# Computing the products with w_up by seven block products instead of eight

## The chip, the core and the metric

The kernel runs on one core of one Trainium2 chip. A core has a matrix engine (TensorE, PE in the profile, with its weight loads as PEld), three engines for elementwise work (VectorE or DVE, ScalarE or ACT, GpSimd or POOL) and a queue that starts the transfers (SyncE or SP). Each engine works off its own list of instructions in order and waits at semaphores for the others. Matrix products are written to PSUM, which has eight banks of 128 partitions x 512 float32; TensorE reads its operands from SBUF. The metric is the time of one execution in device microseconds, lower is better.

## What is computed

One layer of a decoder trunk on 512 tokens of width 1024, all in float32: two gated mixers (a convolution module and a sparse attention), a channel mixer, an embedding gate and a final norm. The change is in the channel mixer:

```
D_MODEL = 1024; SEQ = 512; D_FF = 2816
...
x = x + y @ w_out[i]
hf = rmsnorm(x, norm_ffn[i])
up = causal_dwconv(hf @ w_up[i], ffn_dw_w[i], ffn_dw_b[i])     # w_up: (1024, 2 * 2816), a conv of three taps
gate, val = jnp.split(up, 2, axis=-1)
x = x + (jax.nn.gelu(gate) * val) @ w_down[i]
```

`hf @ w_up` has 512 rows and 5632 columns, that is 44 chunks of 128 columns: 22 of gates (f) and 22 of values (22 + f).

## The kernel before

**Products in two parts.** A product of float32 operands is made from parts: each operand is cut into a `hi` part (a copy rounded to the engine's float32r, by ACT, helper `hi_of`, line 107) and a `lo` part (what is left, by DVE, helper `lo_of`, line 110). Three matmuls then stand for one: hi x hi, hi x lo, lo x hi (`mm_w` at lines 117 to 119 with the weights as the stationary operand, `mm_a` at 123 to 125 with the activations as the stationary operand).

**The weights' stream.** Weights arrive in pieces of 128 x 1024 float32 (512 KB) in the order of their use. `Stream.pump` asks for the next pieces (two raw buffers, `wraw`, started from SP) and starts to cut those that were asked for earlier, into one of four buffers `whl`. `Stream.work` runs the next stage of a cut, `take` hands a cut piece to the products, `done` gives its buffer back. So cuts of later pieces stand in ACT's and DVE's lists between the evacuations of earlier products.

**Around the channel mixer.** `rows_product` makes 512 x 1024 results as row tiles of 128 tokens (t) and column halves (n); `residual` adds them to the rows `x2`. With w_out, the second half runs row tile by row tile: after a tile's product comes its norm (`Norm`: squares on ACT, the power on POOL, the scaled row `hrow` on DVE), and one tile later eight transposes on TensorE (`to_T`, line 341) whose two results of 128 x 512 are cut into `hfT`. After the last tile a product with w_ple (`ple_half`, 24 matmuls) stands between its norm and its transposes.

**The channel mixer.** `up_chunk` (line 1161) makes one chunk of 128 columns for all 512 tokens: eight k steps of three matmuls of 512 columns into one bank. ACT takes it out with the conv's last tap and its bias (line 1170), DVE adds the two other taps, which read the bank (1171, 1172). For a pair, a gate's chunk and a value's, there follow gelu (ACT, 1180), the product (DVE, 1182) and the cut of the result into `a`. Pairs run in groups of 8, 8 and 6; after a group the product with its rows of w_down is made. POOL has nothing to do in the channel mixer.

Of the kernel before, what the change touches and what calls it, by code (L numbers as in the profile page):

```python
# [11 lines left out]
F32R = mybir.dt.float32r  # L12
# [29 lines left out]
# heads whose scores, two units ahead, and whose weights, one unit ahead, are due in a unit's steps  # L42
# [41 lines left out]
def block_kernel(ctx: ExitStack, tc: tile.TileContext, x, p, rel_bias, norm_mix, w_in, conv_dw_w, conv_dw_b,  # L84
# [9 lines left out]

    ctx.enter_context(tc.manual_schedule())
# [4 lines left out]
    def work(name, shape, dtype=F32, tag=None, bufs=1):  # L100
        return sb.tile(list(shape), dtype, name=name, tag=tag or name, bufs=bufs)
# [7 lines left out]
    def lo_of(dst, src, hi):  # L109
        nc.vector.tensor_tensor(dst, src, f32(hi), op=ALU.subtract)  # L110
# [4 lines left out]
    # out += W.T a  with W's parts as the stationary operand  # L115
# [5 lines left out]
    # out += a.T W  with the activations' parts as the stationary operand  # L121
# [6 lines left out]
    # A piece lands as fp32 and is cut into an exact (hi, lo) pair of float32r parts, some pieces ahead of its use.  # L128
# [7 lines left out]

    def rows_pieces(name, w, ks):
        for n in range(2):
            for i in range(0, len(ks), 2):
                nk = len(ks[i:i + 2])  # L140
                pieces.append(((name, n, ks[i]), [cols(w, ks[i], nk, 512 * n, 512)], nk, 512, "whl"))

    def ple_piece(n):
        pieces.append((("ple", n), [cols(w_ple, 0, 2, 512 * n, 512)], 2, 512, "accX"))
# [8 lines left out]
    CMP_AFTER = CMP_AT                      # the compression's eight pieces follow the z pieces from this one on  # L153
# [9 lines left out]
    rows_pieces("out", w_out, list(range(KC)))  # L163
    FFN_GROUPS = ((0, 8), (8, 16), (16, NF))
    for f0, f1 in FFN_GROUPS:
        for f in range(f0, f1):
            for c in (f, NF + f):
                pieces.append((("up", c), [cols(w_up, 0, KC, c * P, P)], KC, P, "whl"))
        if f1 == NF:
            ple_piece(1)  # L170
        rows_pieces("down%d" % f0, w_down, list(range(f0, f1)))
# [4 lines left out]
    class Stream:  # L176
        limit, parts = CUT, 1
        dmas = cuts = taken = raws = wholes = hls = call = 0

        def __init__(self):  # L180
            self.raw, self.hl, self.asked, self.stages = {}, {}, {}, []

        def pump(self, force=False):
# [3 lines left out]
            while self.cuts < self.dmas and (force or self.asked[self.cuts] < self.call):  # L187
                i = self.cuts
                key, _, a, b, tag = pieces[i]
                if tag is not None:  # L190
# [6 lines left out]
                    self.raws -= 1  # L197
                self.cuts += 1
            while self.dmas < len(pieces):
                i = self.dmas  # L200
                key, srcs, a, b, tag = pieces[i]
                if (self.wholes if tag is None else self.raws) == 2:
                    break
                raw = work("wraw", (P, a, b), tag="pT" if tag is None else "wraw", bufs=2)
# [6 lines left out]
                self.raws += tag is not None  # L211
# [21 lines left out]
        def take(self, *key):  # L233
            i = self.taken
# [1049 lines left out]
```

## Time and profile before

| | |
|---|---|
| time, median of 3 runs | 837.78 us (837.27 to 838.08) |
| span of the profiled execution | 835.6 us (its own time beside the span is not given apart; the median lies 2.2 us above the span) |
| TensorE's granted clock | at its full level in all 40 slices of the page |
| matmuls | 3872, of these 1056 with w_up |

The page gives each engine's busy time. A matmul's own duration is longer than the distance to the next, since they are pipelined, so what one costs in a row of many is read from the starts of the first and the last. An engine's idle time is put down to what released it. Transfers ran at a mean of 101 GB/s, and in no wait of TensorE in the channel mixer was a transfer named.

### The profile page before, as it was taken

The page shows a single profiled execution, that of the slowest core. Times are in us where ns is not written, and L with a number is a line of the kernel's source. Part 1 is how long each engine was busy: PE and PEld are TensorE (multiplying, and loading weights), DVE is VectorE, ACT ScalarE, POOL GpSimd, SP SyncE. Part 2 cuts the span into 40 slices and gives each one's busy share as a digit, 9 for nine tenths or more (in the row PEclk, how much of TensorE's full clock was granted, in tenths as well). Part 3 has the DMA queues.
Part 4 walks back from the last instruction along what each step waited for, and adds up shares of the span by engine and source line. Part 5 has one row for each costly group of instructions (what it writes and reads, how often), then busy time and mean ns, then how long its engine had stood idle before and what let it go on. Part 6 is the DMA issues. An engine that isn't in the chain of part 4 may idle for free.

```text
span 835.6 us, 10144 instructions
## 1 busy us (share of the span) xinstructions
PE 821.3 (98%) x3872; PEld 669.0 (80%) x3872; DVE 539.6 (65%) x907; ACT 375.4 (45%) x677; POOL 24.7 (3%) x71
## 2 busy tenths in 40 slices
PE   7999999999999999999999999999999999999996
PEld 6888888888888886888788888888888888888885
DVE  6379977988987897935566663355654356655564
ACT  6332524287778874432544441234442123433443
POOL 2000000000010000001000000000000000001012
PEclk9999999999999999999999999999999999999999
DMA  7347787411110116430333324232333323341312
GB/s 217 83 112 202 165 188 173 96 51 51 51 51 27 51 52 219 134 101 26 100 101 102 93 85 125 80 94 81 99 100 102 101 75 102 102 147 55 120 32 101
DMA packets 108026, 84.54 MB, mean 101 GB/s; under 512 B 4080, under 2 KB 93608, under 8 KB 107978
## 3 DMA queue, kind: packets, MB, share of 16 engines
q1 hardware_dynamic: 107978, 83.90, 35.5%
q8 instruction: 30, 0.49, 0.3%
q14 instruction: 18, 0.15, 0.1%
HBM read 79.36 MB, written 2.43 MB: 98 GB/s over the span
## 4 chain that ended last, share of the span: by engine, by line
PE 96%; ACT 1%; DVE 1%; DMA 1%; issue 0%; POOL 0%; SPq 0%; POOLq 0%; ACTq 0%
PE ps L117 19%; PE ps L119 19%; PE ps L118 19%; PE ps L123 9%; PE ps L124 9%; PE ps L125 9%; PE ps L759 2%; PE ps L785 2%; PE ps L565 2%; PE ps L704 1%; PE ps L705 1%; PE ps L341 1%; PE ps L713 1%; DMA vraw<-in_w_in 1%; PE ps L803 0%
## 5 line engine op out<-in xcount | busy, mean ns | idle before, releaser
L110 DVE TENSOR_TENSOR whl<-wraw,whl 128x1024 fp32r<-128x1024 f32 (+1 forms) x159 | 155.6, 987 | 146.8 <-ACT whl L107 143.7
L107 ACT ACTIVATE whl<-wraw 128x1024 fp32r<-128x1024 f32 (+1 forms) x159 | 133.7, 862 | 124.2 <-PE ps L125 94.3
L117 PE MATMUL ps<-hfT,whl 128*128 128x512 f32 x352 | 139.1, 395 | 0.3 <-ACT hfT L107 0.3
L118 PE MATMUL ps<-hfT,whl 128*128 128x512 f32 x352 | 139.1, 395 | 0.2 <-DVE hfT L110 0.2
L119 PE MATMUL ps<-hfT,whl 128*128 128x512 f32 x352 | 139.0, 395 | 0.0
L117 PE MATMUL ps<-hT,whl 128*128 128x512 f32 x256 | 102.8, 402 | 0.0
L119 PE MATMUL ps<-hT,whl 128*128 128x512 f32 x256 | 101.1, 395 | 0.3 <-DVE whl L110 0.3
L118 PE MATMUL ps<-hT,whl 128*128 128x512 f32 x256 | 100.9, 394 | 0.0
L625 DVE SCALAR_TENSOR_TENSOR acc<-aT,convw,acc 128x512 f32<-128x512 f32 x120 | 86.2, 746 | 1.0
L118 PEld LDWEIGHTS ps<-hfT,whl 128*128 128x128 f32 x352 | 66.2, 188 | 16.4 <-DVE hfT L110 0.5
L117 PEld LDWEIGHTS ps<-hfT,whl 128*128 128x128 f32 x352 | 66.2, 188 | 16.2 <-ACT hfT L107 0.5
L119 PEld LDWEIGHTS ps<-hfT,whl 128*128 128x128 f32 x352 | 66.2, 188 | 15.9
L123 PE MATMUL ps<-whl,a 128*128 128x512 f32 x176 | 69.7, 396 | 0.0
L125 PE MATMUL ps<-whl,a 128*128 128x512 f32 x176 | 69.5, 395 | 0.0
L124 PE MATMUL ps<-whl,a 128*128 128x512 f32 x176 | 69.5, 395 | 0.0
L1170 ACT ACTIVATE up<-ps,ffnw 128x512 f32<-128x512 f32 x44 | 34.3, 780 | 61.5 <-PE ps L119 61.5
L1171 DVE SCALAR_TENSOR_TENSOR up<-ps,ffnw,up 128x511 f32<-128x511 f32 x44 | 33.0, 750 | 43.9 <-ACT up L1170 43.8
L119 PEld LDWEIGHTS ps<-hT,whl 128*128 128x128 f32 x256 | 48.2, 188 | 12.0 <-DVE whl L110 0.7
L117 PEld LDWEIGHTS ps<-hT,whl 128*128 128x128 f32 x256 | 48.2, 188 | 9.9 <-issue 0.2
L118 PEld LDWEIGHTS ps<-hT,whl 128*128 128x128 f32 x256 | 48.3, 189 | 9.4
L125 PEld LDWEIGHTS ps<-whl,a 128*128 128x128 f32 x176 | 33.0, 188 | 8.0
L123 PEld LDWEIGHTS ps<-whl,a 128*128 128x128 f32 x176 | 33.1, 188 | 7.9
(191 smaller groups left out, 1263.6 us busy)
## 6 DMA issues: line engine op xcount, KB each, us to landing
wraw<-in_w_up SPq DMA_DIRECT2D x44, 512.0 KB
wraw<-in_w_in SPq DMA_DIRECT2D x32, 512.0 KB
wraw<-in_w_down SPq DMA_DIRECT2D x22, 512.0 KB
wraw<-in_w_out SPq DMA_DIRECT2D x8, 512.0 KB
wraw<-in_w_ple_gate SPq DMA_DIRECT2D x8, 512.0 KB
W<-vdram SPq DMA_DIRECT2D x8, 264.0 KB
xin<-in_x SPq DMA_DIRECT2D x4, 512.0 KB
wraw<-in_w_ck SPq DMA_DIRECT2D x4, 512.0 KB
```

What stands on the lines that cost most here:

```text
L107: nc.scalar.activation(dst, src, AF.Copy, scale=scale)
L110: nc.vector.tensor_tensor(dst, src, f32(hi), op=ALU.subtract)
L117: nc.tensor.matmul(o, hl[:, 0, j, cs], a_hi, start=start, stop=False)
L118: nc.tensor.matmul(o, hl[:, 0, j, cs], a_lo, start=False, stop=False)
L119: nc.tensor.matmul(o, hl[:, 1, j, cs], a_hi, start=False, stop=stop)
L123: nc.tensor.matmul(o, a_hi, w_hi, start=start, stop=False)
L124: nc.tensor.matmul(o, a_hi, w_lo, start=False, stop=False)
L125: nc.tensor.matmul(o, a_lo, w_hi, start=False, stop=stop)
L565: nc.tensor.matmul(hid_ps[kv][hf], raw[:, jj, hf * P:(hf + 1) * P], Xw[kv][j // 8][:, :, s0:s0 + 16 * (NCMP - 1) + 1:16], start=j == 0, st ...
L625: nc.vector.scalar_tensor_tensor(acc[:, c, :], a[:, k:k + S], convw[:, 4 * k + c:4 * k + c + 1], acc[:, c, :], op0=ALU.mult, op1=ALU.add)
L1170: nc.scalar.activation(u, o, AF.Identity, scale=fw(2, c), bias=fw(3, c))
L1171: nc.vector.scalar_tensor_tensor(u[:, 1:], o[:, :S - 1], fw(1, c), u[:, 1:], op0=ALU.mult, op1=ALU.add)
```

## The change

Two chunks of a pair, a gate's and a value's, are seen as one product of 2 x 2 blocks: the tokens in two halves of 256, the 1024 inner elements in two halves of 512, and the two chunks as the columns. Plain, it has eight block products. Strassen's form (in Winograd's arrangement) has seven, named m1 to m7, and takes sums as operands:

- of the activations: s1 = a21 + a22, s2 = s1 - a11 (DVE), s3 = a11 - a21, s4 = a12 - s2 (POOL), where a21 is the second token half's first inner half. They are made once, on rows, before the transposes. Instead of two transposed results for each of four row tiles there are two for each of tiles 0 and 1 and five for each of tiles 2 and 3.
- of the weights, for every pair: t1 and t2 (`add` "a"), t4 and t3 (`add` "b"), four subtractions of 128 x 512 on POOL. A pair's two raw pieces of 512 KB give four pieces to cut: "11" (128 x 1024), "t12", "t34" (sums, 128 x 1024 each) and "22" (128 x 512, whose `lo` part is made by POOL, but for two of the pairs).
- of the results: a block product that is needed in several outputs is made once, and ACT copies the partial sum between PSUM banks, or between halves of one, before other block products are added: copies after m1, m6, m7 and a "seed" of the gate's bank, 128 x 256 each; m5's result goes to SBUF (`e`), and DVE adds it to both halves of the value (`v`).

A block product is four k steps of three matmuls of 256 columns. A pair in the loop's steady state has the slots m6, m2, m1 of the next pair, m7, m5 of the next pair, m3, m4. Behind each slot stands a stage of a weight's cut and a step of the earlier pair's evacuation (`after`): the two chunks' taps, gelu, product and cut. The value's two taps now read `v` in SBUF, and its first tap too. The copies' waits: m7 waits for the copy of m6 (two slots between), m4 for that of m7 (two slots), m2 for the seed (three slots), m6 for the copy of m1.

The groups are now 7, 7 and 8 pairs, and a group's product with w_down comes inside the second pair after it. Gates and values keep two banks each for all pairs, so four banks are left for the rest. Buffers of the mixers and of the channel mixer are now in two pools, one after the other. The piece of w_ple is asked for after w_out's.

Core of the diff (the bookkeeping of buffers, the loop's first pair and the last stage's changed names are left out):

```diff
+    def mm_block(o, hl, j0, a, start):
+        for k in range(4):
+            nc.tensor.matmul(o, hl[:, 0, j0 + k, :], a[:, 0, k, :], start=start and k == 0, stop=False, skip_group_check=True)
+            nc.tensor.matmul(o, hl[:, 0, j0 + k, :], a[:, 1, k, :], start=False, stop=False, skip_group_check=True)
+            nc.tensor.matmul(o, hl[:, 1, j0 + k, :], a[:, 0, k, :], start=False, stop=k == 3, skip_group_check=True)
...
-    FFN_GROUPS = ((0, 8), (8, 16), (16, NF))
+    FFN_GROUPS = ((0, 7), (7, 14), (14, NF))
...
+    for f in range(1, NF):
+        if f + 1 < NF:
+            up_raw(f + 1)
+            up_sums(("a", f + 1), ("b", f + 1), ("11", f + 1))
...
+        up_sums(("t34", f))
+        if f + 1 < NF:
+            up_sums(("t12", f + 1))
+        up_sums(("22", f))
...
+                    self.cut(hl, src, a, nc.gpsimd if key[0] == "22" and key[1] not in DOWN_IN else nc.vector)
...
+            sub = lambda to, x_, y_: nc.gpsimd.tensor_tensor(to, x_, y_, op=ALU.subtract)
+            if name == "a":
...
+                sub(t1, at("12"), at("11"))
+                sub(t2, at("22"), t1)
...
+            else:
+                sub(to[:, 4:8], at("21"), at("t2"))
+                sub(to[:, 0:4], at("22"), at("12"))
...
+        nc.vector.tensor_tensor(s1, a21, a22, op=ALU.add)
+        nc.vector.tensor_tensor(s2, s1, a11, op=ALU.subtract)
+        nc.gpsimd.tensor_tensor(s3, a11, a21, op=ALU.subtract)
+        nc.gpsimd.tensor_tensor(s4, a12, s2, op=ALU.subtract)
...
+        def m1(self):
+            self.b1 = st.take("11", self.f)
+            mm_block(self.extra[:, HI], self.b1, 0, hf["a11"], True)
+            nc.scalar.activation(self.value[:, HI], self.extra[:, HI], AF.Copy)
+        def seed_gate(self):
+            nc.scalar.activation(self.gate[:, LO], self.value[:, HI], AF.Copy)
+        def m5(self):
+            self.t12 = st.take("t12", self.f)
+            mm_block(self.extra[:, LO], self.t12, 0, hf["s1"], True)
+            self.e = work("m5", (P, 256), tag="sc", bufs=2)
+            nc.scalar.activation(self.e, self.extra[:, LO], AF.Copy)
+        def m6(self):
+            mm_block(self.value[:, HI], self.t12, 4, hf["s2"], False)
+            nc.scalar.activation(self.value[:, LO], self.value[:, HI], AF.Copy)
+        def m2(self):
+            mm_block(self.gate[:, LO], self.b1, 4, hf["a12"], False)
+        def m7(self):
+            self.t34 = st.take("t34", self.f)
+            mm_block(self.value[:, HI], self.t34, 0, hf["s3"], False)
+            nc.scalar.activation(self.gate[:, HI], self.value[:, HI], AF.Copy)
+        def m3(self):
+            b22 = st.take("22", self.f)
+            mm_block(self.value[:, LO], b22, 0, hf["s4"], False)
+        def m4(self):
+            mm_block(self.gate[:, HI], self.t34, 4, hf["a22"], False)
...
+            nc.vector.tensor_tensor(halves(v), halves(self.value), self.e.unsqueeze(1).broadcast_to((P, 2, 256)),
+                                    op=ALU.add)
...
+            nc.scalar.activation(ug, self.gate, AF.Identity, scale=fw(2, f), bias=fw(3, f))
+            yield
+            nc.scalar.activation(uv, v, AF.Identity, scale=fw(2, c), bias=fw(3, c))
+            self.taps(ug, self.gate, f)
+            yield
+            nc.scalar.activation(ug, ug, AF.Gelu_apprx_tanh)
+            self.taps(uv, v, c)
```

How the lists stand. First DVE's, for one pair in the middle of the channel mixer; `whl` are weights' cuts (the `lo` part), `up` the two chunks' taps, `a` the cut of the pair's result. Before:

```order
L110 TENSOR_TENSOR whl_4585<-wraw_4525,whl_4585 128x1024
L1171 SCALAR_TENSOR_TENSOR up_4615<-ps_4589,ffnw0_816,up_4615 128x511
L1172 SCALAR_TENSOR_TENSOR up_4615<-ps_4589,ffnw0_816,up_4615 128x510
L110 TENSOR_TENSOR whl_4620<-wraw_4554,whl_4620 128x1024
L1171 SCALAR_TENSOR_TENSOR up_4650<-ps_4624,ffnw0_816,up_4650 128x511
L1172 SCALAR_TENSOR_TENSOR up_4650<-ps_4624,ffnw0_816,up_4650 128x510
L1182 TENSOR_TENSOR up_4650<-up_4615,up_4650 128x512
L110 TENSOR_TENSOR a_4655<-up_4650,a_4655 128x512
```

The same place now; `tt` are the weights' sums, `ug` and `uv` the gate's and the value's chunk, `m5` the result of m5 in SBUF:

```order
L121 TENSOR_TENSOR whl_5597<-wraw_5343,whl_5597 128x1024
L121 TENSOR_TENSOR whl_5614<-tt_5416,whl_5614 128x1024
L121 TENSOR_TENSOR whl_5630<-tt_5541,whl_5630 128x1024
L121 TENSOR_TENSOR a_5591<-uv_5465,a_5591 128x512
L1359 SCALAR_TENSOR_TENSOR ug_5594<-ps_3344,ffnw0_819,ug_5594 128x511
L1359 SCALAR_TENSOR_TENSOR ug_5594<-ps_3344,ffnw0_819,ug_5594 128x510
L1359 SCALAR_TENSOR_TENSOR uv_5593<-v_5595,ffnw0_819,uv_5593 128x511
L1359 SCALAR_TENSOR_TENSOR uv_5593<-v_5595,ffnw0_819,uv_5593 128x510
L1379 TENSOR_TENSOR uv_5593<-ug_5594,uv_5593 128x512
L1366 TENSOR_TENSOR v_5723<-ps_3345,m5_5575 128x512
```

Eight instructions a pair have become ten: a third cut of 128 x 1024 and the sum `v` have come, and the value's two taps read SBUF (`v`) where they read a bank (`ps`).

POOL's list has no row in the channel mixer before. Now it has these for every pair; here they are for one pair, and the first of the next:

```order
L307 TENSOR_TENSOR tt_5541<-wraw_5393,wraw_5343 128x512
L307 TENSOR_TENSOR tt_5541<-wraw_5393,tt_5541 128x512
L307 TENSOR_TENSOR tt_5544<-wraw_5343,tt_5541 128x512
L307 TENSOR_TENSOR tt_5544<-wraw_5393 128x512
L121 TENSOR_TENSOR whl_5647<-wraw_5265,whl_5647 128x512
L307 TENSOR_TENSOR tt_5669<-wraw_5521,wraw_5471 128x512
```

Five two-operand instructions of 128 x 512 a pair have come to POOL, all with both operands in SBUF. ACT's list for a pair went from six instructions (two cuts of 128 x 1024, two takings-out, gelu, the cut of `a`) to thirteen: the cut of "11", of "t34", m6's copy, the cut of "t12", the gate's taking-out, the cut of "22", m1's copy, the value's first tap, m7's copy, gelu, m5's copy, the seed, the cut of `a`, in this order.

## Rows read from the trace of the kernel before

**Rows 1.** The page: span, and each engine's busy time, share and instructions
```profile
span 835.6 us, 10144 instructions
...
PE 821.3 (98%) x3872; PEld 669.0 (80%) x3872; DVE 539.6 (65%) x907; ACT 375.4 (45%) x677; POOL 24.7 (3%) x71
```

**Rows 2.** Waits of PE, 380 to 836: in total, times, longest (us)
```profile
PE ps L117 <- ACT hfT L107: 0.3, 1, 0.3
PE ps L118 <- DVE hfT L110: 0.2, 1, 0.2
```

**Rows 3.** Windows: busy us (instructions) per engine, clock, DMA share, GB/s
```profile
560.00:650.00 90.00, 90.00 (x387) 72.39 (x386) 51.46 (x60) 33.90 (x42) 0.00 (x0) 1.00 0.32 96
```

**Rows 4.** Timeline of PE, w_up products: start, duration, line, operands
```profile
560.04 0.39 PE L118 MATMUL ps<-hfT,whl 128*128 128x512 f32 x1
...
574.98 0.39 PE L119 MATMUL ps<-hfT,whl 128*128 128x512 f32 x1
```

**Rows 5.** Timeline of PE, 256-column products at the end
```profile
822.08 0.28 PE L123 MATMUL ps<-whl,hpT 128*128 128x256 f32 x1
...
827.65 0.28 PE L125 MATMUL ps<-whl,hpT 128*128 128x256 f32 x1
```

**Rows 6.** Timeline of PE, a row tile's transposes (L341) between products
```profile
383.50 1.03 PE L341 MATMUL ps<-ci,hrow 128*128 128x128 f32 x8
384.29 0.47 PE L123 MATMUL ps<-whl,y 128*128 128x512 f32 x1
384.61 0.39 PE L124 MATMUL ps<-whl,y 128*128 128x512 f32 x1
```

**Rows 7.** Lines by form, 500 to 836: busy us, mean ns, idle before
```profile
L110 DVE TENSOR_TENSOR whl<-wraw,whl 128x1024 fp32r<-128x1024 f32 x56 | 68.5, 1224 | 94.2 <-ACT whl L107 94.1
...
L107 ACT ACTIVATE whl<-wraw 128x1024 fp32r<-128x1024 f32 x55 | 57.8, 1052 | 85.0 <-PE ps L125 84.1 <-DMA wraw<-in_w_down 1.0
...
L1170 ACT ACTIVATE up<-ps,ffnw 128x512 f32<-128x512 f32 x28 | 21.8, 780 | 40.1 <-PE ps L119 40.1
...
L1171 DVE SCALAR_TENSOR_TENSOR up<-ps,ffnw,up 128x511 f32<-128x511 f32 x28 | 21.0, 750 | 28.6 <-ACT up L1170 28.5
...
L1137 DVE TENSOR_TENSOR x<-ps,x 128x512 f32<-128x512 f32 x24 | 16.1, 686 | 7.6 <-PE ps L125 7.6
...
L110 DVE TENSOR_TENSOR a<-up,a 128x512 fp32r<-128x512 f32 x14 | 9.7, 693 | 9.8 <-ACT a L107 9.8
...
L107 ACT ACTIVATE a<-up 128x512 fp32r<-128x512 f32 x14 | 8.9, 633 | 32.6 <-DVE up L1182 32.6
...
L1180 ACT ACTIVATE up<-up 128x512 f32<-128x512 f32 x14 | 8.8, 632 | 23.2 <-DVE up L1172 23.2
...
L1207 ACT ACTIVATE pg<-ps 128x256 f32<-128x256 f32 x2 | 0.7, 374 | 0.4 <-PE ps L125 0.4
```

**Rows 8.** Timeline of POOL: small operations of the norms
```profile
757.52 0.21 POOL L318 TENSOR_SCALAR ss<-ss 128x1 f32<-128x1 f32 x1 [1.15 <-ACT junk L314]
...
807.79 2.86 POOL L318 TENSOR_SCALAR ss<-ss 128x1 f32<-128x1 f32 x4 [27.30 <-ACT junk L314]
...
814.13 0.63 POOL L327 TENSOR_TENSOR rstd<-ss 128x1 f32<-128x1 f32 x1 [3.48 <-ACT junk L314]
```

**Rows 9.** Timeline of DVE beside them
```profile
757.39 0.69 DVE L1137 TENSOR_TENSOR x<-ps,x 128x512 f32<-128x512 f32 x1 [0.71 <-PE ps L125]
...
808.70 2.49 DVE L1250 TENSOR_TENSOR x<-x,gain 128x512 f32<-128x512 f32 x4
...
814.02 0.69 DVE L1221 TENSOR_TENSOR x<-x,gain 128x512 f32<-128x512 f32 x1 [0.85 <-ACT junk L314]
```

**Rows 10.** Lines by form of POOL, whole span: its two widest memsets
```profile
L510 POOL MEMSET VC<- 32x256 f32 x1 | 0.3, 303 | 0.0
...
L509 POOL MEMSET KCt<- 128x128 f32 x1 | 0.2, 205 | 0.0
```

More of the change, by code (lines that the diff above doesn't have):

```diff
@@ L233, in take @@
         def take(self, *key):
+            while pieces[self.taken][4] in ("first", "second", "add"):
+                self.taken += 1
             i = self.taken
             assert pieces[i][0] == key, (pieces[i][0], key)
-            if i == self.cuts - 1:
+            if i >= self.cuts - 2:
                 while self.stages:
@@ L1065, in block_kernel @@
     yT = {}
-    x2 = work("x2", (P, NT, D), tag="B", bufs=2)
-    for t in range(NT):
-        nc.sync.dma_start(x2[:, t, :], x_rows[t])
     for m2 in range(4):
@@ L1107, in rows_product @@
                 between()
-            for t in range(NT):
+            before = None
+            for t in order:
                 if t == NT - 1 and last:
@@ L1147, in block_kernel, with ready, out_done @@
     gain_f = load_gain(norm_ffn)
-    hfT = work("hfT", (P, 2, KC, S), F32R, tag="A", bufs=1)
-    hl_ple = st.take("ple", 0)
     for t in range(NT):
         p_parts(t)
+    for t in range(NT):
+        nc.sync.dma_start(x2[:, t, :], x_rows[t])
+    pairs = {}
+    def ready(t):
+        norms[t].rows(halves=True)
+        row_sums(t)
+    def out_done(t, n, o):
+        residual(t, n, o, gain_f)
+        if n and t != 3:
+            ready(t)
+        if n and t == 1:
+            st.adds = 1
@@ new lines, in out_late, with before_last @@
+    def out_late(t):
+        turn_halves(t, ROWS_FIRST if t == 2 else EVERY)
+        if t == 1:
+            turn_halves(2, ("s3", "s4", "a22"))
+    def before_last():
+        ready(3)
+        st.adds = len(pieces)
+        st.pump()
+        ple_half(0)
+        st.work()
+        st.pump()
+        pairs[0] = Pair(0)
+        pairs[0].m1()
+        st.work()
+        st.pump()
+        turn_halves(3, ("s1",))
+        pairs[0].seed_gate()
+        pairs[1] = Pair(1)
+        pairs[1].m1()
+        st.work()
+        st.pump()
+        turn_halves(3, ("s2",))
+        pairs[1].seed_gate()
@@ new lines, in block_kernel, with step, slot, down @@
+                 banks=lambda n, t: (gates + values)[t] if n else ps(), order=(0, 2, 1, 3), cut_on=True)
+    tails = []
+    def step():
+        for tail in list(tails):
+            if next(tail, tails) is tails:
+                tails.remove(tail)
+    def slot(product, cut=True):
+        product()
+        st.work()
+        step()
+        if cut:
+            st.pump()
+    def down(f0, f1, gain, *late, **kw):
+        rows_product("down%d" % f0, list(range(f0, f1)),
+                     lambda k, t: (act[k][:, 0, t * P:(t + 1) * P], act[k][:, 1, t * P:(t + 1) * P]),
+                     lambda t, n, o: residual(t, n, o, gain), *late, **kw)
@@ new lines, in drain @@
+    def drain():
+        while tails:
+            step()
+    for f in range(NF):
+        this, coming = pairs[f], pairs.get(f + 1)
+        if f == 0:
+            slot(this.m5)
+            turn_halves(3, ("s3",))
+            slot(coming.m2)
+            slot(this.m6)
+            turn_halves(3, ("s4",))
+            slot(coming.m5)
+            turn_halves(3, ("a22",))
+            slot(this.m7)
+            slot(this.m2)
+        else:
+            cut = f not in DOWN_IN
+            slot(this.m6, cut)
+            if f > 1:
+                slot(this.m2, cut)
+            else:
+                step()
+            if f + 1 < NF:
+                coming = pairs[f + 1] = Pair(f + 1)
+                slot(coming.m1, cut)
+            if f in DOWN_IN:
+                step()
+                st.pump(most=1)
+                step()
+                st.work()
+                drain()
+                down(*DOWN_IN[f], None, banks=lambda n, t: ps() if t < 3 else coming.gate)
+            slot(this.m7)
+            if f + 1 < NF:
+                slot(coming.m5)
+                coming.seed_gate()
+        tails.append(this.after())
+        slot(this.m3)
+        slot(this.m4)
@@ L1199, in block_kernel @@
+    drain()
+    gain_p = load_gain(norm_ple)
+    hpT = [work("hpT", (P, 2, KC, P), F32R, tag="hf", bufs=7) for t in range(NT)]
+    down(*FFN_GROUPS[-1], gain_p, lambda t: norms[t].to_T(hpT[t], 0), lambda: ple_half(1))
     gain_o = load_gain(norm_final)
```

272 lines of the change are left out of this document (188 added, 84 removed).

## The prediction

> **What bounds the kernel now.** I read the engines' busy time first, then what TensorE waited for, then a stretch of the channel mixer, then the timeline of single instructions. TensorE is busy for 98% of the span [rows 1]; the reader is to see that no other engine comes near. From the last norm of the mixers to the end it waited in two places, 0.5 us together, both where the transposed rows are first cut [rows 2]. In 90 us of the w_up stage it was busy for all 90, at a granted clock of 1.00 (the 2.4 GHz level), with DVE at 51.5, ACT at 33.9 and POOL at nothing [rows 3]. So this stage takes what its matmuls take, one after the other, and only what shortens that row, or makes it wait, changes the time.
>
> **The matmuls.** 512 columns: 64 steps from 560.04 to 574.98, 0.2334 us each [rows 4]. 256 columns: the last tile of the final product has 48 of them in a row with a new weight for each; 47 steps from 822.08 to 827.65 are 0.1185 us each [rows 5], which is 0.508 of the long one, so loading a weight for every 256 columns is hidden. Removed: 44 chunks x 24 = 1056 x 0.2334 = 246.5 us. Added: 22 pairs x 7 x 12 = 1848 x 0.1185 = 219.0 us. **-27.5 us**. A pair falls from 11.20 to 9.95 us, a slot is 1.42.
>
> **The transposes.** Eight take 0.79 us (383.50 to 384.29), and the product behind them needs 0.32 to its next where 0.23 is usual [rows 6]: 0.88 for eight, 0.44 for a set of four. Sets go from 8 to 14: **+2.6 us**, all on TensorE.
>
> **The entry.** Behind the last row tile of w_out's product the norm's chain is longer by two DVE sums of 0.69 (the 128 x 512 form of [rows 7]); beside them stand two new m1 slots, 2.84 us, in addition to the 24 matmuls with w_ple that cover the chain today but for 0.5 us [rows 2]. Between nothing and 2.8 (both sums and a first cut, late in full); I take **+1.0**.
>
> **The copies.** I set a pair at 0 with its m6 and put ACT's thirteen instructions in their order with the durations of [rows 7] (1.052 a cut of 128 x 1024, 0.633 one of 128 x 512, 0.780 a taking-out, 0.632 gelu, 0.374 for 128 x 256 out of a bank, the nearest row for a copy into one). The cut of "t34" begins when m4 of the pair before gives its buffer back, at 0, and ends at 1.1; m6's copy runs 1.5 to 1.9, m7 needs it at 4.26. The cut of "t12" ends at 2.95, its `lo` part on DVE (1.224) at 4.2, m5 needs it at 5.69. Gate out to 3.7, cut of "22" to 4.4; m1's copy to 4.7; value's tap to 5.5; m7's copy to 6.1, needed by m4 at 8.53; gelu to 6.8; m5's copy to 7.5, seed to 7.9, `a` to 8.5, and the cut of the next "11" follows. That is 8.48 us of work in 9.95, and no product is kept waiting: the least room is 2.3 us for a copy and 1.5 for a cut. **0** while ACT isn't held up; what it costs when it is, is a rival below. Four free banks in place of eight for w_down's products: a bank is emptied by one DVE add (0.686 [rows 7]) while the other tiles' last products run; nothing, or up to 2 us over three groups. Transfers: the same bytes, 96 GB/s in [rows 3] becomes 108, no wait for one today; nothing. The order of pieces on SP's queue changes (x2 and w_ple later), with a whole product ahead of their use; nothing.
>
> **DVE and POOL.** DVE's ten instructions a pair: 3 x 1.224 + 4 x 0.750 + 2 x 0.693 + 0.686 = 8.74 us of 9.95 (before 6.83 of 11.20). That fits alone. But POOL now works beside it, and the two touch: a POOL operation of one element takes 0.21 us while DVE adds from a bank to SBUF; the same form takes 2.86 us for four while DVE multiplies two SBUF operands, and one that begins at 814.13 during such a DVE instruction ends at 814.76, just behind its end at 814.71 [rows 8, 9]. So POOL stands still while DVE reads two operands from SBUF. The other direction no row shows: DVE's four keep 0.6 us from one to the next, but POOL's work there is one element.
>
> By that, port time adds up. DVE's share with two SBUF operands is 3 x 1.224 + 2 x 0.750 (the value's taps, which now read `v`) + 2 x 0.693 = 6.56 us a pair. POOL's five two-operand instructions of 128 x 512 have no row. Bounds: memsets of 256 and 128 elements differ by 98 ns, 0.77 ns an element on top of 0.106 us [rows 10]; one such stream of 512 is 0.50 us, three one after the other (two reads, a write) 1.29. The nearest row of the same form is DVE's 0.693, which I take: 6.56 + 5 x 0.69 = 10.0 us, just over TensorE's 9.95. As the pieces won't fit without gaps I add 0.25 us a pair: **+5.5 us**. At 0.50 the sum is 9.06 and it costs nothing; at 1.29 it is 13.0 and costs 3.05 x 22 = 67.
>
> The Trainium skill (SBUF — State Buffer, Who interferes with whom) states this rule: a Vector instruction with two SBUF inputs and a GpSimd instruction that reads SBUF share a port, the one that comes first keeps it for its whole length and the other is fully blocked. The trace agrees for POOL; for DVE it shows nothing. The Trainium skill (GPSIMD Engine Reference, Performance versus the Vector engine) gives 4497 ns for a two-input add of 2048 elements; a quarter of it, 1.12 us, is an estimate for these, and by it the port's sum would be 12.2 us a pair and the time 862 us.
>
> **The sum.** -27.5 + 2.6 + 1.0 + 5.5 = -18.4 us on the span of 835.6: 817.2. The median of the runs stood 2.2 above that span, so I forecast **819.5 us**, 2.2% less.
>
> **Rivals.**
> 1. *The port becomes the bound; slower.* Speaks for it: [rows 8, 9], and DVE at 88% leaves POOL 3.4 us of free port a pair. Against it: no row shows DVE waiting for POOL, and POOL's price is open. At 1.09 us an instruction (half way between two streams, 0.89, and three, 1.29) a pair takes 6.56 + 5.45 = 12.0 us, 2.06 over TensorE's: +45.3 in place of +5.5, **859 us**. The place to see it: POOL's sums come late, ACT's cut of "t12" or "t34" waits for them, m6's copy stands behind that cut, and m7 and m5 behind both. It decides from (27.5 - 3.6) / 22 = 1.09 us a pair on, a pair of 11.04 us, a POOL instruction of 0.90.
> 2. *ACT's list holds the copies back; about even.* ACT has 1.5 us a pair to spare, and its cuts wait for buffers, sums and transfers in order. If one cut's length (1.05) is lost on TensorE in every pair, 22 x 1.05 = 23.1: 813.9 + 23.1 = **837 us**. For it: thirteen instructions with ten of them waiting for other engines. Against it: the least room of 1.5 us above.
> 3. *Nothing waits at all.* POOL at 0.50 us, no loss at the entry: 837.8 - 27.5 + 2.6 = **813 us**; the lower end of the forecast.
>
> **Chances.** Forecast with rival 3 as its lower end 0.45 (its own range 812 to 828, from no loss to 0.65 us a pair); rival 2 0.20, spread over 826 to 845; rival 1 0.35, from 838 to the 880 that 1.29 gives. A measurement of this kernel can tell 0.2% (1.7 us) from no change. Faster: 0.45 and half of rival 2, 0.55; within: 0.06 of rival 2 and 0.01 of rival 1; slower: 0.04 and 0.34. The range runs from 812 to 860, where it leaves out the upper half of rival 1 (0.16) and a little below.
>
> **What will show it.** Right: matmuls of 256 columns 0.1185 us apart within a slot, pairs of 10.0 to 10.4 us, hardly a wait on a copy. The port: DVE's 128 x 1024 cuts longer than 1.22 us where POOL runs, POOL's instructions of 128 x 512 near 0.7 (forecast) or above 0.9 (rival 1), TensorE's waits put down to cuts of "t12" or "t34". ACT: waits put down to the copies after m6, m7 or the seed while POOL is early. Wrong altogether: a 256-column matmul that comes slower than 0.12 us when its bank was just written by ACT, which no row of before has.

## The result, and the profile after

The changed kernel takes **858.15 us** (median of four runs, 857.31 to 860.02), the kernel before 837.93 beside it: a ratio of 1.0248, 95% interval 1.0233 to 1.0262. Slower by 20.2 us, where 819.5 and a gain were forecast. The time lies inside the stated range (812 to 860), but the kernel moved the other way; the figure of rival 1, 859 us, is what came.

The page of the kernel after answers to [rows 1]. TensorE has less work (811.9 us in place of 821.3) and is no longer all of the chain: a quarter of the chain that ended last is DVE's, and in that stand the lines 1359 and 1379 (the taps, and gelu's product with the value), whose counterparts (1171, 1172 and 1182) were not on it before.

```profile
span 855.3 us, 12272 instructions
...
PE 811.9 (95%) x4688; PEld 702.5 (82%) x4688; DVE 633.2 (74%) x965; ACT 441.8 (52%) x839; POOL 202.3 (24%) x183
...
PE 66%; DVE 24%; ACT 4%; issue 3%; POOL 1%; DMA 1%; SPq 0%; POOLq 0%; DVEq 0%; ACTq 0%
```

The same row of the kernel before:

```profile
PE 96%; ACT 1%; DVE 1%; DMA 1%; issue 0%; POOL 0%; SPq 0%; POOLq 0%; ACTq 0%
```

The window of [rows 3], the same 90 us of the w_up stage. TensorE works for 83.3 of 90, DVE for 75.9 (51.5 before), POOL for 47.7 (nothing before). The granted clock is 0.96; from 700 to 724 us it was 1.00 and a pair just as long, and in e2 below it was 1.00 in such windows and the time longer, so it isn't the cause.

```profile
560.00:650.00 90.00, 83.34 (x607) 78.97 (x606) 75.89 (x72) 53.05 (x89) 47.67 (x30) 0.96 0.31 90
```

What TensorE waited for between 370 and 860 us, which answers to [rows 2] (in total, times, longest). The two large groups are cuts of weights: `lo` parts by DVE and `hi` parts by ACT. Copies between banks (L1345) are 1.0 us, POOL 0.6:

```profile
PE ps L137 <- DVE whl L121: 11.3, 17, 1.4
PE ps L135 <- ACT whl L118: 9.5, 11, 2.0
PE ps L136 <- DVE hf L121: 2.0, 1, 2.0
PE ps L1299 <- DVE hsum L1284: 1.4, 1, 1.4
PE ps L1299 <- DVE hf L121: 1.3, 1, 1.3
PE ps L1299 <- DVE hhalf L442: 1.3, 2, 1.0
PE ps L135 <- ACT ps L1345: 1.0, 2, 0.5
PE ps L137 <- POOL whl L121: 0.6, 1, 0.6
```

Now one pair in the steady state, 12.11 us from one "22" on POOL to the next (9.95 was worked out for TensorE). First POOL (start, duration, line, operands; the bracket is the wait before): five instructions of 128 x 512, a `lo` cut and four sums.

```profile
467.38 1.83 POOL L121 TENSOR_TENSOR whl<-wraw,whl 128x512 fp32r<-128x512 f32 x1 [3.92 <-ACT whl L118]
469.16 1.31 POOL L307 TENSOR_TENSOR tt<-wraw 128x512 f32<-128x512 f32 x1
470.55 3.33 POOL L307 TENSOR_TENSOR tt<-wraw,tt 128x512 f32<-128x512 f32 x2
473.83 1.74 POOL L307 TENSOR_TENSOR tt<-wraw 128x512 f32<-128x512 f32 x1
479.49 1.83 POOL L121 TENSOR_TENSOR whl<-wraw,whl 128x512 fp32r<-128x512 f32 x1 [3.91 <-ACT whl L118]
```

DVE in the same pair. The gate's two taps read a bank: 1.53 us for both. The value's two are the same instruction, but read `v` in SBUF: 3.31 us, and the product of two SBUF operands behind them 1.60, where the same product took 0.69 before.

```profile
467.36 0.68 DVE L121 TENSOR_TENSOR a<-uv,a 128x512 fp32r<-128x512 f32 x1
467.96 1.53 DVE L1359 SCALAR_TENSOR_TENSOR ug<-ps,ffnw,ug 128x511 f32<-128x511 f32 x2
469.41 3.31 DVE L1359 SCALAR_TENSOR_TENSOR uv<-v,ffnw,uv 128x511 f32<-128x511 f32 x2
472.82 1.60 DVE L1379 TENSOR_TENSOR uv<-ug,uv 128x512 f32<-128x512 f32 x1
474.35 0.68 DVE L1366 TENSOR_TENSOR v<-ps,m 128x512 f32<-128x512 f32 x1
476.07 1.23 DVE L121 TENSOR_TENSOR whl<-wraw,whl 128x1024 fp32r<-128x1024 f32 x1 [1.04 <-ACT whl L118]
```

ACT waits 3.69 us for that product, and the cut of the next "11" stands behind it in its list, though its data are there:

```profile
470.39 0.38 ACT L1325 ACTIVATE ps<-ps 128x256 f32<-128x256 f32 x1
474.46 0.63 ACT L118 ACTIVATE a<-uv 128x512 fp32r<-128x512 f32 x1 [3.69 <-DVE uv L1379]
475.00 1.04 ACT L118 ACTIVATE whl<-wraw 128x1024 fp32r<-128x1024 f32 x1
```

And TensorE, whose matmuls of 256 columns come 0.12 us apart [rows 5] until m1 wants that cut, twice (its `hi`, then its `lo` part):

```profile
474.93 0.28 PE L136 MATMUL ps<-hf,whl 128*128 128x256 f32 x1
475.05 0.28 PE L137 MATMUL ps<-hf,whl 128*128 128x256 f32 x1
476.09 0.39 PE L135 MATMUL ps<-hf,whl 128*128 128x256 f32 x1 [0.76 <-ACT whl L118]
...
477.35 0.39 PE L137 MATMUL ps<-hf,whl 128*128 128x256 f32 x1 [0.76 <-DVE whl L121]
```

From start to start the two stops are 1.04 us each where 0.12 is usual, and the matmul behind each comes 0.10 late: 2.0 us, all that separates a pair from its 84 matmuls (84 x 0.120 = 10.08).

So the reading was: DVE is held by POOL for 2.7 us a pair (3.31 - 1.53 and 1.60 - 0.69), ACT's list by DVE, the cut by ACT's list, TensorE by the cut. That is **theory P**. Rivals: the five copies on ACT hold its list by themselves (A), TensorE's new slots are longer than costed (C), the sums come too late for their cuts (rival 1's own place).

### The profile page after: what moved, and what is told of

It reads as the page before. It is cut to its first block, busy times and chain, and to the rows that moved or that the text cites. A ratio compares the mean times of both kernels' runs of the same rounds, so it can differ in the third digit from the quotient of the medians.

```text
span 855.3 us, 12272 instructions
## 1 busy us (share of the span) xinstructions
PE 811.9 (95%) x4688; PEld 702.5 (82%) x4688; DVE 633.2 (74%) x965; ACT 441.8 (52%) x839; POOL 202.3 (24%) x183
## 4 chain that ended last, share of the span: by engine, by line
PE 66%; DVE 24%; ACT 4%; issue 3%; POOL 1%; DMA 1%; SPq 0%; POOLq 0%; DVEq 0%; ACTq 0%
PE ps L128 9%; PE ps L130 9%; PE ps L129 8%; PE ps L142 8%; PE ps L141 8%; PE ps L143 8%; DVE whl L121 8%; DVE uv L1359 6%; DVE uv L1379 3%; ACT whl L118 3%; DVE ug L1359 3%; PE ps L869 2%; PE ps L895 2%; PE ps L675 2%; PE ps L137 1%
## 5 line engine op out<-in xcount | busy, mean ns | idle before, releaser
L121 DVE TENSOR_TENSOR whl<-wraw,whl 128x512 fp32r<-128x512 f32 (+1 forms) x140 | 130.6, 945 | 107.4 <-ACT whl L118 107.1
L137 PE MATMUL ps<-hf,whl 128*128 128x256 f32 x616 | 178.9, 290 | 12.0 <-DVE whl L121 11.3
L135 PE MATMUL ps<-hf,whl 128*128 128x256 f32 x616 | 178.4, 290 | 10.6 <-ACT whl L118 9.5
L136 PE MATMUL ps<-hf,whl 128*128 128x256 f32 x616 | 176.6, 287 | 2.0 <-DVE hf L121 2.0
L118 ACT ACTIVATE whl<-wraw 128x512 fp32r<-128x512 f32 (+1 forms) x160 | 123.5, 794 | 94.1 <-PE ps L143 43.0
L137 PEld LDWEIGHTS ps<-hf,whl 128*128 128x128 f32 x616 | 120.4, 195 | 16.1 <-DVE whl L121 15.2
L135 PEld LDWEIGHTS ps<-hf,whl 128*128 128x128 f32 x616 | 120.3, 195 | 13.3 <-ACT whl L118 11.8
L136 PEld LDWEIGHTS ps<-hf,whl 128*128 128x128 f32 x616 | 120.4, 195 | 2.3 <-DVE hf L121 2.2
L307 POOL TENSOR_TENSOR tt<-wraw 128x512 f32<-128x512 f32 x44 | 66.0, 1500 | 81.0 <-DVE whl L121 76.9
L307 POOL TENSOR_TENSOR tt<-wraw,tt 128x512 f32<-128x512 f32 x44 | 71.7, 1629 | 9.2 <-DVE whl L121 6.0
L121 DVE TENSOR_TENSOR whl<-tt,whl 128x1024 fp32r<-128x1024 f32 x44 | 54.9, 1278 | 23.1 <-ACT whl L118 23.1
L1359 DVE SCALAR_TENSOR_TENSOR uv<-v,ffnw,uv 128x511 f32<-128x511 f32 (+1 forms) x44 | 63.3, 1439 | 1.1 <-ACT uv L1373 0.3
L118 ACT ACTIVATE whl<-tt 128x1024 fp32r<-128x1024 f32 x44 | 46.0, 1046 | 22.4 <-PE ps L143 19.0
L130 PEld LDWEIGHTS ps<-hT,whl 128*128 128x128 f32 x256 | 48.1, 188 | 11.3 <-DVE whl L121 0.7
L128 PEld LDWEIGHTS ps<-hT,whl 128*128 128x128 f32 x256 | 48.1, 188 | 9.0 <-issue 0.2
```

Source lines behind the costliest of these rows:

```text
L118: nc.scalar.activation(dst, src, AF.Copy, scale=scale)
L121: engine.tensor_tensor(dst, src, f32(hi), op=ALU.subtract)
L128: nc.tensor.matmul(o, hl[:, 0, j, cs], a_hi, start=start, stop=False)
L130: nc.tensor.matmul(o, hl[:, 1, j, cs], a_hi, start=False, stop=stop)
L135: nc.tensor.matmul(o, hl[:, 0, j0 + k, :], a[:, 0, k, :], start=start and k == 0, stop=False, skip_group_check=True)
L136: nc.tensor.matmul(o, hl[:, 0, j0 + k, :], a[:, 1, k, :], start=False, stop=False, skip_group_check=True)
```

## The experiments

Each ran beside the kernel before on its chip (837.4 to 837.9 us); ratios are to that. "Pair" is the distance between two of a kernel's "22" cuts on POOL.

**1. e1_no_sums: POOL's sums left out.** From the second pair on the cuts take the first pair's sums; POOL keeps the "22" cut.

```diff
         def add(self, name, f):
+            if f > 0:
+                if name == "a":
+                    self.sums["t12", f] = self.tt[0], self.call + 1
+                else:
+                    self.sums["t34", f] = self.tt[1], self.call + 1
+                return
```

> Leaves out the four weight subtractions on POOL of every pair but the first (the first pair's sums are cut again for each later pair, so that every cut, copy, matmul and tap stays). POOL keeps one instruction of five a pair. Theory P (POOL's reads of two SBUF operands and DVE's shut each other out, and DVE's lateness reaches PE): a pair falls from 12.11 us to 10.0 to 10.4 us, the time to 812 to 821 us, the uv taps L1359 from 1.42 back to about 0.75 us and the product L1379 from 1.39 to about 0.7 us. Rival A (ACT's strict list with its five new copies holds the cuts back): nothing on ACT changes, the time stays at 850 to 858 us. Rival C (PE's own slots of 256-column matmuls are longer than costed): stays at 850 to 858 us too.

820.1 us, ratio 0.979 (0.9775 to 0.9804). On DVE the value's taps are back at those of the gate, the product at 0.69:

```profile
569.21 1.53 DVE L1366 SCALAR_TENSOR_TENSOR ug<-ps,ffnw,ug 128x511 f32<-128x511 f32 x2
570.66 1.52 DVE L1366 SCALAR_TENSOR_TENSOR uv<-v,ffnw,uv 128x511 f32<-128x511 f32 x2
572.29 0.69 DVE L1386 TENSOR_TENSOR uv<-ug,uv 128x512 f32<-128x512 f32 x1
```

Of TensorE's waits from 380 to 840 us those for w_up's cuts are gone. What is left stands at the entry, but for one copy's 0.5 us and 0.6 us at a product with w_down (left out here):

```profile
PE ps L136 <- DVE hf L121: 2.0, 1, 2.0
PE ps L1306 <- DVE hsum L1291: 1.4, 1, 1.4
PE ps L135 <- ACT ps L1352: 1.0, 2, 0.5
PE ps L1306 <- DVE hf L121: 0.9, 1, 0.9
...
PE ps L1306 <- ACT whl L118: 0.2, 1, 0.2
```

A pair is 10.08 us, which is 84 matmuls 0.120 us apart. A and C fall: all of ACT's copies and all slots are there. The four sums cost 38 us.

**2. e6_unread and e7_unread_one: the sums made, but read by nobody.** The cuts take the first pair's sums as above; POOL still computes, in the second run with one operand in place of two.

```diff
-                self.sums["t12", f] = to, self.call + 1
+                self.sums["t12", f] = self.kept, self.call + 1
...
-                self.sums["t34", f] = to, self.call + 1
+                self.sums["t34", f] = to if f == 0 else self.kept, self.call + 1
```

The run with one operand has this beside it:

```diff
-            sub = lambda to, x_, y_: nc.gpsimd.tensor_tensor(to, x_, y_, op=ALU.subtract)
+            def sub(to, x_, y_):
+                if f == 0:
+                    nc.gpsimd.tensor_tensor(to, x_, y_, op=ALU.subtract)
+                else:
+                    nc.gpsimd.tensor_scalar(to, x_, -1.0, None, op0=ALU.mult)
```

> POOL makes all its four weight subtractions a pair, as in the kernel after, but from the second pair on nobody reads them: the cuts take the first pair's sums (so the output is another), as in the run without sums, which took 820.1 us. So no cut waits for POOL, and only what POOL does to its neighbours is left. Theory P (POOL stretches DVE's instructions beside it): 845 to 862 us. A theory that the sums come too late for the cuts (POOL's 1.3 to 1.8 us each in a row): 818 to 824 us.

> As the run with unread sums, but each of the four POOL instructions a pair reads one SBUF operand of 128x512 and not two (times -1, nobody reads the result). If it is POOL's and DVE's second SBUF operands that shut each other out, DVE's instructions return to 0.69 to 0.75 and 1.22 us beside them, and the time to 818 to 826 us. If any POOL work on SBUF holds DVE, 835 to 860 us.

860.0 us (ratio 1.0268, 1.0251 to 1.0285) and 826.3 us (0.9874, 0.9856 to 0.9892), the second 0.3 us above the range it was given. So it isn't late sums, but what POOL does to its neighbours: in e6 the value's taps still take 1.6 to 1.7 us each and the product 1.6. And it goes with the second operand; the instruction's form changes with it (TENSOR_SCALAR for TENSOR_TENSOR), and no run here tells the two apart. In e7 POOL is busy longer than in the kernel after, 1.8 us an instruction (its timeline, four of them):

```profile
587.86 7.18 POOL L313 TENSOR_SCALAR tt<-wraw 128x512 f32<-128x512 f32 x4
```

Yet on DVE beside it the value's two taps take 1.70 us and the product 0.91:

```profile
588.09 1.70 DVE L1365 SCALAR_TENSOR_TENSOR uv<-v,ffnw,uv 128x511 f32<-128x511 f32 x2
589.90 0.91 DVE L1385 TENSOR_TENSOR uv<-ug,uv 128x512 f32<-128x512 f32 x1
```

A pair there mostly takes 9.83 us and 11.53 by turns, and in one of the two the cut of `a` on DVE meets POOL's "22" cut, the one instruction with two operands that e7 keeps, and takes 1.78 us.

**3. e2_banks: fewer DVE instructions with two SBUF operands.**

```diff
-            uv, ug, v = [work(name, (P, 512), tag="S", bufs=8) for name in ("uv", "ug", "v")]
+            uv, ug = [work(name, (P, 512), tag="S", bufs=8) for name in ("uv", "ug")]
+            v = self.value
...
-            nc.scalar.activation(ug, ug, AF.Gelu_apprx_tanh)
+            nc.scalar.activation(self.gate, ug, AF.Gelu_apprx_tanh)
...
-            nc.vector.tensor_tensor(uv, ug, uv, op=ALU.mult)
+            nc.vector.tensor_tensor(uv, self.gate, uv, op=ALU.mult)
```

The sum `v` is now written in place into the value's bank, and its taps read it there, two steps after the sum.

> All sums stay on POOL. The sum v is written in place into the value's PSUM bank, the value's taps read it there (two steps after the sum, before the bank is wanted by pair f+2), and gelu writes into the gate's bank, so that three DVE instructions a pair (two uv taps, one product) read one operand from SBUF and not two. Theory P: DVE's work with two SBUF operands falls from 6.54 to 4.35 us a pair, with five POOL instructions at 1.11 to 1.30 us the port's sum is 9.9 to 10.9 us, a pair 10.0 to 11.2 us, the time 812 to 838 us; uv taps about 0.75 us. A theory that DVE has simply too much work, or that POOL's instructions are too slow by themselves (5 x 1.6 us, fed in time for neither cut), expects 850 us or more, since no instruction is taken away.

865.5 us (1.0336, 1.032 to 1.0351): slower still, and outside what theory P allowed. It lies where the other theories expected it (850 or more), but e1 and e6 speak against both: DVE's instructions are all there in e1 at 820.1 us, and in e6 nobody reads the sums and it is as slow as the change. The taps did come down to 0.75 us each and the product to 0.69. But POOL's five now met the cut of "t12" and the cut of `a` on DVE:

```profile
470.63 2.25 DVE L121 TENSOR_TENSOR whl<-tt,whl 128x1024 fp32r<-128x1024 f32 x1
472.80 1.77 DVE L121 TENSOR_TENSOR a<-uv,a 128x512 fp32r<-128x512 f32 x1
474.50 1.52 DVE L1359 SCALAR_TENSOR_TENSOR ug<-ps,ffnw,ug 128x511 f32<-128x511 f32 x2
```

Behind these two stand the gate's taps, and on ACT gelu waits 4.64 us for them:

```profile
476.12 0.60 ACT L1378 ACTIVATE ps<-ug 128x512 f32<-128x512 f32 x1 [4.64 <-DVE ug L1359]
```

The cut of the next "11" stands behind gelu in ACT's list. A pair is 12.93 us, though the sum of what needs the port is smaller by 2.2 us. **A sum over the port doesn't give the time.** Nor is it, with the durations of the rows, a floor: 6.56 + 5 x 1.30 = 13.1 us where the change's pair took 12.11, and 4.37 + 6.5 = 10.9 where e8_a_lo below takes 10.33.

**4. e3_a_late and e4_dve2.** The first moves the `hi` cut of `a` one slot down ACT's list, behind the cut of "11"; the second gives two of POOL's five instructions to DVE.

```diff
+            yield
             hi_of(a[:, 0], uv)
-            yield
```
```diff
-                    self.cut(hl, src, a, nc.gpsimd if key[0] == "22" and key[1] not in DOWN_IN else nc.vector)
+                    self.cut(hl, src, a, nc.vector)
...
-                sub(to[:, 0:4], at("22"), at("12"))
+                nc.vector.tensor_tensor(to[:, 0:4], at("22"), at("12"), op=ALU.subtract)
```

> The only edit: the hi cut of the activation a on ACT stands one slot later in ACT's list, behind the cut of the coming block 11, which waited behind it in the kernel after. If the port costs time only because a late product (DVE) holds ACT's strict list and with it the cut of 11 (PE then waits 0.76 us twice a pair), a pair falls to 10.9 to 11.5 us and the time to 831 to 845 us, with the uv taps still stretched at about 1.4 us. If the port itself is full (6.54 us of DVE and 5 x 1.1 us of POOL in 12.1 us), another order gives nothing: 852 to 860 us, and PE waits the same sum at another cut.

> Two of POOL's five instructions a pair (the lo cut of block 22 and the sum 22 minus 12) go to DVE, at some 0.69 us each there. Theory P: the port holds 6.54 + 1.38 us of DVE and 3 x 1.11 to 1.30 us of POOL, 11.25 to 11.8 us a pair, 839 to 851 us. Were DVE's amount of work the bound, and not the port, 1.4 us a pair more on DVE would make it slower by up to 30 us, 870 to 888 us. Rival A (ACT's list alone): 858 us as before.

e3: 853.3 us (1.0185, 1.0167 to 1.0204). TensorE's wait for ACT's cuts is gone, but that for DVE's went from 11.3 to 20.5 us, and DVE is busy for 58.7 of 60 us with instructions that POOL stretches: a small gain, in the range that was expected of a full port (852 to 860). e4: 870.2 us (1.0391, 1.0374 to 1.0409), 12 us slower with two POOL instructions fewer, against theory P, and at the lower end of what DVE's amount of work as the bound was given (870 to 888). The `lo` cut of "22" had run on POOL beside the gate's taps, which read a bank and stayed at 1.53 us for both; on DVE it takes 1.76 us in place of 0.69, held by POOL's sums like the cut of `a` ahead of it, with the gate's taps behind both:

```profile
473.40 1.79 DVE L121 TENSOR_TENSOR a<-uv,a 128x512 fp32r<-128x512 f32 x1
475.12 1.76 DVE L121 TENSOR_TENSOR whl<-wraw,whl 128x512 fp32r<-128x512 f32 x1
```

The value's taps and the product are back at 1.53 and 0.69 us, so DVE is held for 2.2 us a pair where it was 2.7; but it has 1.4 us more to do. Its own work counts as well as the holds.

**Theory L.** What decides is which DVE instruction stands beside each POOL instruction, and what stands behind it: DVE's and ACT's strict lists make a loop once a pair (cut, taps, gelu, product, next cut), and each hold on it, and each instruction added to it, lengthens the pair. The next four runs test it.

**5. e5_spread and e5_spread_dve1: the loop loosened.** As e2, with gelu two slots behind the gate's taps, `a`'s cut two behind the product, the value's taps a slot later, and m1's copy and the seed moved to the slots of m5 and m4 (the seed then reads m1's own bank); the second also has the "22" cut on DVE.

```diff
             self.taps(ug, self.gate, f)
             yield
+            yield
             nc.scalar.activation(self.gate, ug, AF.Gelu_apprx_tanh)
...
-                coming.seed_gate()
+                coming.copy_m1()
         slot(this.m3)
         slot(this.m4)
+        if f and f + 1 < NF:
+            coming.seed_gate()
```

> All sums on POOL; banks as in the run e2 (taps and product read one operand from PSUM), and the steps of a pair stand further apart in the lists of ACT and DVE: gelu two slots behind the gate's taps, the hi cut of a two behind the product, the copy of m1 into the value's bank and the gate's seed moved to the slots of m5 and m4, so that ACT is not held by DVE and cuts block 11 in time. Theory L (the loss comes by a loop through both strict lists: DVE late, ACT held, the next cut late; e2 lost there 4.6 us of ACT and 2.4 us of DVE a pair): DVE's own 8.74 us and the 2.1 us that POOL stretched in e2 make 10.9 to 11.2 us a pair, 828 to 838 us. If the port is full whatever the order (12.1 us of it), 852 us or more.

> As e5_spread, and the lo cut of block 22 on DVE (0.69 us there), so that POOL has four instructions a pair. Theory L: DVE 9.43 us and a stretch of 1.3 to 2.1 us, 10.7 to 11.5 us a pair, 825 to 845 us; a port that is full whatever the order: 0.4 to 0.6 us a pair less than e5_spread, some 10 us faster than it.

845.7 us (1.0097, 1.0082 to 1.0112) and 874.9 us (1.0445, 1.0429 to 1.046). The first lies between the two theories' figures: 19.8 us under e2 with the same instructions, but above 838. Its pair is 11.41 us. The second missed both: 30 us above what theory L gave it, and 29 above e5_spread, where the full port expected it some 10 below. Its pair is 13.07 us, 1.66 more: the cut's own 0.69 and a hold of 1.03. Its DVE rows show two holds ahead of the gate's taps:

```profile
487.00 1.72 DVE L121 TENSOR_TENSOR whl<-wraw,whl 128x512 fp32r<-128x512 f32 x1
488.65 1.77 DVE L121 TENSOR_TENSOR a<-uv,a 128x512 fp32r<-128x512 f32 x1
490.34 1.52 DVE L1363 SCALAR_TENSOR_TENSOR ug<-ps,ffnw,ug 128x511 f32<-128x511 f32 x2
```

In e5_spread itself one such hold was left ahead of the gate's taps. POOL's first sum there:

```profile
573.58 1.30 POOL L307 TENSOR_TENSOR tt<-wraw 128x512 f32<-128x512 f32 x1
```

DVE begins `a`'s cut 0.10 us behind it and is held to its end, between the taps; and further down DVE waits 1.08 us for ACT, where that cut would cost nothing:

```profile
573.68 1.75 DVE L121 TENSOR_TENSOR a<-uv,a 128x512 fp32r<-128x512 f32 x1
575.35 1.52 DVE L1363 SCALAR_TENSOR_TENSOR ug<-ps,ffnw,ug 128x511 f32<-128x511 f32 x2
...
582.50 1.23 DVE L121 TENSOR_TENSOR whl<-tt,whl 128x1024 fp32r<-128x1024 f32 x1 [1.08 <-ACT whl L118]
```

**6. e8_a_lo and b1_before_pool.** The one moves that cut into that gap; the other adds four POOL subtractions a pair, read by nobody, to the kernel before, whose DVE has room.

```diff
             hi_of(a[:, 0], uv)
-            yield
-            yield
             lo_of(a[:, 1], uv, a[:, 0])
```
```diff
             lo_of(act[f][:, 1], uv, act[f][:, 0])
+            for i in range(4):
+                nc.gpsimd.tensor_tensor(uv, uv, f32(hfT[:, 0, i, :]), op=ALU.subtract)
```

> e5_spread (845.7 us) with one edit: the lo cut of a on DVE stands right behind its hi cut, between the lo cuts of t34 and t12, where DVE waited 0.9 to 1.1 us for ACT, and no longer between the taps, where POOL's first sum held it for 1.06 us and the gate's taps, gelu (2.0 us of ACT's wait) and the next cut of block 11 behind it. Theory L (an instruction is held for what is left of the one that POOL has begun, and this counts only on the path through both lists): a pair falls from 10.9 to 11.4 us to 10.2 to 10.7 us, the time to 822 to 835 us, under the kernel before. If only the port's sum counts, the same instructions in another order give 843 to 848 us.

> The kernel before, with four POOL subtractions of 128x512 with two SBUF operands added for each pair of chunks, behind the lo cut of a; nobody reads what they write (uv, which is done with). Theory L: they take some 1.3 us each and hold the lo cut of a weight chunk beside them by 0.5 to 1.3 us, but DVE is busy for only 6.4 of 11.2 us a pair and its cuts stand ahead of their need, so the time stays at 837 to 842 us. If such POOL work costs by itself what it cost in the changed kernel (820.1 to 858.2 us with the sums, 38 us), 865 to 876 us.

e8_a_lo: **831.3 us**, ratio 0.9916 (0.9896 to 0.9937), a pair of 10.33 us: under the kernel before, with all of POOL's sums and the same port sum as e2 (865.5). The cut of `a` is no longer held; the cut of "t34" ahead of it still is:

```profile
470.60 2.31 DVE L121 TENSOR_TENSOR whl<-tt,whl 128x1024 fp32r<-128x1024 f32 x1
472.83 0.68 DVE L121 TENSOR_TENSOR a<-uv,a 128x512 fp32r<-128x512 f32 x1
```

b1_before_pool: 837.75 us, ratio 1.000 (0.9991 to 1.0009). Its weight cuts on DVE went from 1.22 us [rows 7] to a mean of 1.68 and TensorE waited no more than in [rows 2]:

```profile
L110 DVE TENSOR_TENSOR whl<-wraw,whl 128x1024 fp32r<-128x1024 f32 x56 | 93.7, 1680 | 87.2 <-ACT whl L107 86.8 <-PE ps L119 0.3
```

So such POOL work is free where DVE's list has room ahead of its need, and it cost 38 us where it hasn't. Both expectations of theory L held.

**7. e9_sum_first and e10_seed: the last quarter of a microsecond.** e9 lets the younger pair's steps go first in a slot (DVE had waited 0.73 us a pair for gelu with the next `v` behind it); e10 puts the seed before the cut of "t34" as well (the first edit below is in both, the move of the seed is e10's).

```diff
-        for tail in list(tails):
+        for tail in list(tails)[::-1]:
...
         slot(this.m3)
+        if f and f + 1 < NF:
+            coming.seed_gate()
         slot(this.m4)
-        if f and f + 1 < NF:
-            coming.seed_gate()
```

> e8_a_lo (831.3 us) with the steps of the younger pair ahead of the older's in each slot: on DVE the sum v of pair f+1 stands ahead of the product of pair f, which waited there 0.73 us a pair for gelu, and on ACT the value's identity ahead of the hi cut of a. In e8_a_lo DVE is the bound of a pair (10.32 us: 9.6 us of instructions and that 0.73 us). Theory L: a pair of 9.95 to 10.1 us and then PE is the bound, 821 to 827 us. If the wait only moves (the cut of a comes later and t12's lo behind it), 829 to 834 us.

> e9_sum_first (830.3 us) with the copy that seeds the gate's bank put one slot earlier in ACT's list, ahead of the cut of t34 and no longer behind it. In e9_sum_first a pair was 10.33 us where 84 matmuls 0.120 us apart make 10.08 us, and the one gap that PE's rows show in a pair (0.15 to 0.2 us) ended with that copy. If it is the bound's last 0.25 us, a pair is 10.08 to 10.12 us and the time 823 to 827 us. If DVE (some 9.6 us a pair) or POOL (8.8 us) bind instead, 829 to 832 us.

830.3 us (0.9919, 0.9906 to 0.9933) and **828.4 us** (0.9891, 0.9874 to 0.9907). e9 missed theory L's 821 to 827 and is the "wait only moves" of its expectation: DVE now waits 0.81 us for m3, and the pair stays at 10.33:

```profile
476.96 0.70 DVE L1371 TENSOR_TENSOR ps<-ps,m 128x512 f32<-128x512 f32 x1 [0.81 <-PE ps L137]
```

In e10 a pair is 10.22 us in most, 0.14 above the 84 matmuls, and 10.08 in a few; the time is 1.8 us less, hardly more than single runs differ, and the 823 to 827 expected were not reached. It lies 9 us under the kernel before and 30 under the change as made.

## Why the prediction was wrong

**The step that failed is "DVE and POOL".** It priced POOL's 128 x 512 instruction at the nearest row of the same form, DVE's 0.693, and the term at +5.5 us. Where nothing holds it, it takes 1.26 to 1.31 us, about the upper bound that the step had worked out from two memsets (1.29). The term measured 38 us (858.2 less e1's 820.1) for four of the five instructions. With 1.29, the step's own sum said 13.0 us a pair and 67 us: so the price alone doesn't mend it, since the sum over the port is wrong as a model too. e2 and e8_a_lo have the same port sum and lie 34 us apart. What should stand there is the order: which DVE instruction is held, for how long, and who is behind it.

**Rival 1** came out at 859 with a pair of 12.0 against 858.2 and 12.11, partly by chance: its price of 1.09 was too low and its sum over the port too strict, and the two cancelled. Its place was wrong as well. It had ACT's cuts of "t12" and "t34" wait for late sums; from 500 to 760 us of the kernel after, no wait of ACT is put down to POOL, and e6, where nobody reads the sums, is as slow. That DVE waits for POOL, the direction that no row of before showed, is now seen: a 0.69 us cut that begins 0.10 us behind a POOL instruction of 1.30 takes 1.75 (e5_spread). The Trainium skill (SBUF — State Buffer, Who interferes with whom) has two SBUF inputs on DVE contend with a GpSimd instruction that reads SBUF, and calls the ports they share an exclusive lock. That who issues first keeps them for the whole instruction, and the other fully blocks, it says of other DVE instructions (the 2-port modes). The trace shows nearly that here, in both directions: DVE's cut of `a` is held for 1.06 of the 1.20 us that POOL's instruction had left, POOL's "22" cut, begun 0.02 us behind a cut of `a` of 0.68, for 0.53 (it takes 1.83). The page's rule makes no difference by GpSimd's inputs; with one operand (e7) the pair of taps grew by 0.2 us, with two by 1.8. The Trainium skill (GPSIMD Engine Reference, Performance versus the Vector engine) gave the estimate of 1.12 us; measured is about 1.30.

**The matmuls** were right in kind: -27.5 us from 0.1185 us a step. In the stage they come 0.120 apart, so a pair is 10.08 and not 9.95: 1848 x 0.0015 = 2.8 us less gained, -24.7.

**The entry** was too small at +1.0, and its bounds (0 to 2.8) too narrow. TensorE waits there for the sums, the scaled rows and the first cuts: 2.0 + 1.4 + 1.3 and, for the scaled rows, 1.3 in the rows above. Without the four sums of a pair it is 2.0 + 1.4 + 0.9 + 0.2, against 0.5 before: +4.0.

**The copies** at nothing, and the transposes, stand: in e1 the waits of TensorE for copies are 1.0 us in all. Together, 837.8 - 24.7 + 2.6 + 4.0 + 1.0 = 820.7, where e1 measured 820.1. So rival 3's case, with the entry mended, is what the change is worth when POOL is left out of it. **Rival 2** (ACT's list) was not a cost of its own, but the way by which DVE's delay reached TensorE: e1, with every one of ACT's instructions, shows no wait for a cut there.

What stays open: e5_spread and e5_spread_dve1 (845.7 and 874.9) lay above what theory L allowed, and were explained only afterwards, the first by the one hold that e8_a_lo then removed, the second by no further run. Theory L names the holds to look for, but of the times that it gave for the changed kernel only e8_a_lo's came. Open too are the 8 us between e10_seed and e1, of which the pair's 0.14 us explains 3.

## What to carry to other kernels

Work given to an idle POOL is not free work: price it by its own rows, or by the upper bound, and look which DVE instructions with two SBUF operands run beside it. Then don't add up a port, but walk one period through the strict lists: an instruction that is held delays all that is queued behind it, and the next engine's list behind that. Put POOL's bursts beside DVE instructions that read a bank, and held instructions where their list waits anyway; with the same instructions, the order of the lists was worth 34 us here (e2 to e8_a_lo).

## What the runs showed that was not expected

- Fewer POOL instructions made it slower, twice (858.2 to 870.2, 845.7 to 874.9), since the cut that left POOL came into DVE's path with its own 0.69 us and was held there for 1.0 to 1.1 us more by a sum.
- A POOL instruction with one SBUF operand (128 x 512, times a constant) took 1.7 to 1.8 us beside a busy DVE, longer than a subtraction of two that nothing holds (1.30), and yet hardly held DVE: the two taps beside it took 1.70 us in place of 3.31.
- The kernel before took, in its last 336 us, 60 POOL subtractions (94 us of POOL's time) and weight cuts stretched by 37% with no measurable change of its time.
